# Four pairs of k-tiles by seven products, quarters from GpSimd's queue, and 1 KB runs in the gated transposes

## The chip, the cores and the metric

The kernel runs on one core of one Trainium2 chip. The metric is the device time of one execution in microseconds (us). The version before takes 1965.18 us, the median of three runs (1962.07 to 1971.79).

## What is computed

One decoder layer over 256 tokens of width 2048, all in float32: a half-step SwiGLU feed-forward, a mixer (gated DeltaNet beside stick-breaking attention), a second half-step feed-forward, a gated embedding, and a norm. The change lies in the two feed-forwards and at the kernel's start.

```python
def swiglu(x, w_gu, w_down):
    gate, up = jnp.split(x @ w_gu, 2, axis=-1)
    return (jax.nn.silu(gate) * up) @ w_down

h = h + 0.5 * swiglu(rms_norm(h, ffn1_norm[i]), ffn1_w_gu[i], ffn1_w_down[i])   # D 2048, D_FF 5632
h = h + hybrid_mixer(rms_norm(h, mix_norm[i]), ...)
h = h + 0.5 * swiglu(rms_norm(h, ffn2_norm[i]), ffn2_w_gu[i], ffn2_w_down[i])
gate = jax.nn.sigmoid(rms_norm(h, ple_norm[i]) @ ple_w_gate[i])
h = h + gate * (p[i] @ ple_w_proj[i])
return rms_norm(h, final_norm)
```

## The kernel before

**Float32 by three matmuls.** Each float32 operand is split into a high part (ScalarE casts it to fp32r) and a low part (VectorE subtracts the high part). A product is then three matmuls: high by high, high by low, low by high. The activations `nTh`, `nTl` (and `hTh`, `hTl` between the two layers of a feed-forward) are split once. Each weight is split as it arrives.

**Plain pairs.** `weight_pair` loads two k-tiles of a 512-column block into `raw` from SP's queue (four buffers), ScalarE makes `whi` (L70), VectorE makes `wlo` (L71); three buffers each. A pair takes 12 matmuls: two k-tiles, two halves of the 256 tokens, three matmuls.

**Groups.** A feed-forward is done in three parts (`PARTS`: 3, 4 and 4 blocks of 512 of the inner width). A part has one group for each block ("gu": a gate and an up block, eight pairs of k-tiles each) and then two groups of the second layer ("dn": two output blocks each). A group's first `ns` pairs of k-tiles are not done plainly but by seven products (`Group`): the two k-tiles and two token halves on one side, the two k-tiles and two column blocks on the other, form a two-by-two product, which Strassen's and Winograd's scheme does in seven products in place of eight, so 21 matmuls for a pair of both blocks in place of 24. `ns` is 3 in gu groups (`NS`), and 2 or 3 in dn groups (`NS_DOWN`); two gu groups at the start of the first feed-forward and one of the second are all plain.

**The sums.** The weight side of the seven products (`all_sums`) works in four buffers `R`, the quarters, named by k-tile and column block. Each product's operand is split by ScalarE into `shi` (L282) and by VectorE into `slo` (L283), two buffers each. Between products VectorE adds one quarter to another twice (L287), and GpSimd's queue twice adds a quarter from memory onto a buffer with an accumulating DMA (L291). The activation side is made by `halves`, once a part for gu and once for dn: VectorE adds high and low (L396), forms four sums `S` (L403), ScalarE and VectorE split them into `Sh` (L404) and `Sl` (L405). After the third and fourth product ScalarE copies a bank to `part` and VectorE adds it into another (L321, L322).

**What sets the order.** `plan` writes for each group the order of its plain pairs and, between them, the seven products of the group that follows (`at`), and the loads of the quarters of the group after that (`loads`). `next_weights` walks that list and prepares up to two pairs and one sum ahead. Each engine then works through its own instructions in order. Quarters are loaded from SP's queue, in line with the pairs. At the end of a gu group, `down_input` multiplies gate and up (L426), transposes 32 by 32 blocks on VectorE (L165), and sends them through memory (`scr`, `tT`) to finish the transpose; `hTh` and `hTl` are made from it later.

**The start.** `first_loads` fetches the input's transposed tiles `xT` in step with the first group's pairs, then `h` itself. The first group goes through all eight pairs of the gate block and then through those of the up block.

Of the kernel before, what the change touches and what calls it, by code (L numbers as in the profile page):

```python
# [16 lines left out]
P = 128  # L17
T = 256
# [11 lines left out]
NS = 3  # L30
NS_DOWN = tuple(3 if i1 - i0 == 4 else 2 for i0, i1 in PARTS)


W_IN_ORDER = (2, 0, 4, 3, 1, 5, 8, 10, 12, 9, 11, 13, 6, 7)
EPS = 1e-6
# [4 lines left out]
def block_kernel(ctx, tc, a, out):  # L40
# [37 lines left out]
    def next_weights():  # L78

        ahead = min(LEAD, done[1] // 2)  # L80
# [44 lines left out]
    for _ in range(8):  # L125
        nc.tensor.matmul(idle[:, 0:P], zero[:, 0:P], zero[:, 0:P], start=True, stop=True)
# [70 lines left out]
    def norm_block(nT, which, j, tmp):  # L197

        if j < 3:
            lanes.add(0, norm_block_behind(nT, which, j, tmp))  # L200
            return
# [39 lines left out]
    class Group:  # L241
# [89 lines left out]
    def plan(n):  # L331
# [9 lines left out]
        for p, (i0, i1) in enumerate(PARTS):  # L341
            for i in range(i0, i1):
                src = [sources("w_gu" + n, 2 * i + b) for b in range(2)]
                groups.append(Group("gu", p, [x[0] for x in src], [x[1] for x in src], NS if i > (n == "1") else 0,
# [4 lines left out]
        made = []  # L349
        for i, group in enumerate(groups):  # L350
# [3 lines left out]
            at, loads = [], {}  # L354
# [25 lines left out]
    for nb in range(3):  # L380
        order += [("pair", a["w_pp"][nb])] + [("pair", a["w_pg"][nb][g]) for g in range(KD // 2)]
    order.append(("pair", a["w_pp"][3]))

    def halves(kind, his, los, ns, wait=0):
# [5 lines left out]
        sh = fp.tile([P, 4, NS, P], F32R, tag="Sh", name="Sh")  # L390
        sl = fp.tile([P, 4, NS, P], F32R, tag="Sl", name="Sl")
        for g0 in range(0, ns, 2):
            n = min(2, ns - g0)
            hi, lo = his[g0 // 2], los[g0 // 2]
            x = fp.tile([P, 2, 4, P], F32, tag="tT", name="tT").rearrange("p t q y -> p (t q y)")[:, 0:2 * n * T]
# [871 lines left out]
```

## Time and profile before

| what | value |
|---|---|
| median of the runs | 1965.18 us |
| the profiled execution's own time | 1963.91 us |
| its span, first to last instruction | 1962.2 us |
| mean granted TensorE clock | 0.998 |
| share of the chain that ended last: PE | 87% |
| bytes moved by DMA | 468.28 MB, 239 GB/s on average |

The first feed-forward lies at 0 to about 705 us of the span, the mixer up to about 1165 us, the second feed-forward up to about 1855 us. An instruction's duration in the profile holds the latency of its pipeline, so instructions of one engine that follow each other directly start closer together than their durations say; where the rate matters, the distance of starts is taken. In the tables by stage, a window's row has the busy time of PE, PEld, DVE, ACT and POOL with counts in brackets, then the granted clock, the share of the DMA engines' time that is busy, and GB/s.

### The profile page before, as it was taken

The page shows a single profiled execution, that of the slowest core. Times are in us where ns is not written, and L with a number is a line of the kernel's source. Part 1 is how long each engine was busy: PE and PEld are TensorE (multiplying, and loading weights), DVE is VectorE, ACT ScalarE, POOL GpSimd, SP SyncE. Part 2 cuts the span into 40 slices and gives each one's busy share as a digit, 9 for nine tenths or more (in the row PEclk, how much of TensorE's full clock was granted, in tenths as well). Part 3 has the DMA queues.
Part 4 walks back from the last instruction along what each step waited for, and adds up shares of the span by engine and source line. Part 5 has one row for each costly group of instructions (what it writes and reads, how often), then busy time and mean ns, then how long its engine had stood idle before and what let it go on. Part 6 is the DMA issues. An engine that isn't in the chain of part 4 may idle for free.

```text
span 1962.2 us, 24725 instructions
## 1 busy us (share of the span) xinstructions
PE 1942.3 (99%) x8941; PEld 1606.5 (82%) x8941; DVE 1536.1 (78%) x1771; ACT 1152.7 (59%) x1402; POOL 83.7 (4%) x108
## 2 busy tenths in 40 slices
PE   9999999999999999999999999999999999999998
PEld 7888888888888888878888888887888888888887
DVE  6779878897888766797856578888889887798755
ACT  6655656565656567665555456565566555665554
POOL 0000000000000000010100000000000000000000
PEclk9999999999999999999999999999999999999999
DMA  8988888888887765556564788887889878887764
GB/s 298 293 246 249 265 261 254 261 260 245 264 278 241 223 217 164 175 160 222 168 208 155 242 284 244 255 263 247 251 254 292 274 229 240 258 273 246 235 206 148
DMA packets 166554, 468.28 MB, mean 239 GB/s; under 512 B 20640, under 2 KB 59552, under 8 KB 166304
## 3 DMA queue, kind: packets, MB, share of 16 engines
q1 hardware_dynamic: 156352, 418.57, 62.3%
q0 software_dynamic: 8928, 46.67, 13.4%
q8 instruction: 70, 1.15, 0.2%
q10 hardware_dynamic: 1152, 1.47, 0.2%
q14 instruction: 52, 0.43, 0.1%
HBM read 444.62 MB, written 22.02 MB: 238 GB/s over the span
## 4 chain that ended last, share of the span: by engine, by line
PE 87%; DVE 5%; issue 4%; DMA 2%; ACT 1%; POOL 0%; SPq 0%; ACTq 0%; POOLq 0%; DVEq 0%
PE u L472 5%; PE u L473 5%; PE u L471 5%; PE g L472 5%; PE g L473 5%; PE g L471 5%; PE d L472 4%; PE d L473 4%; PE d L471 4%; PE pj L106 3%; PE pj L107 3%; PE pj L105 3%; PE g L315 3%; PE g L316 2%; PE g L314 2%
## 5 line engine op out<-in xcount | busy, mean ns | idle before, releaser
L70 ACT CAST whi<-raw 128x1024 fp32r<-128x1024 f32 (+1 forms) x531 | 557.2, 1051 | 521.5 <-PE d L473 112.4
L71 DVE TENSOR_TENSOR wlo<-raw,whi 128x1024 fp32r<-128x1024 f32 (+1 forms) x531 | 643.3, 1216 | 220.7 <-ACT whi L70 217.6
L283 DVE TENSOR_TENSOR slo<-R,shi 128x1536 fp32r<-128x1536 f32 (+1 forms) x217 | 365.5, 1686 | 126.6 <-ACT shi L282 124.8
L282 ACT CAST shi<-R 128x1536 fp32r<-128x1536 f32 (+1 forms) x217 | 309.6, 1428 | 166.2 <-PE g L316 44.8
L471 PE MATMUL g<-whi,nTh 128*128 128x512 f32 x476 | 185.3, 391 | 2.3 <-ACT whi L70 2.3
L472 PE MATMUL g<-wlo,nTh 128*128 128x512 f32 x476 | 186.4, 392 | 0.5 <-DVE wlo L71 0.5
L473 PE MATMUL g<-whi,nTl 128*128 128x512 f32 x476 | 186.2, 391 | 0.0
L471 PE MATMUL u<-whi,nTh 128*128 128x512 f32 x476 | 185.2, 389 | 0.0
L472 PE MATMUL u<-wlo,nTh 128*128 128x512 f32 x476 | 185.2, 389 | 0.0
L473 PE MATMUL u<-whi,nTl 128*128 128x512 f32 x476 | 185.2, 389 | 0.0
L105 PE MATMUL pj<-whi,nTh 128*128 128x512 f32 x448 | 179.7, 401 | 0.0
L106 PE MATMUL pj<-wlo,nTh 128*128 128x512 f32 x448 | 175.3, 391 | 2.2 <-DVE wlo L71 2.2
L107 PE MATMUL pj<-whi,nTl 128*128 128x512 f32 x448 | 175.0, 391 | 0.0
L472 PE MATMUL d<-wlo,hTh 128*128 128x512 f32 x448 | 174.4, 389 | 0.0
L471 PE MATMUL d<-whi,hTh 128*128 128x512 f32 x448 | 174.3, 389 | 0.0
L473 PE MATMUL d<-whi,hTl 128*128 128x512 f32 x448 | 174.3, 389 | 0.0
L471 PEld LDWEIGHTS g<-whi,nTh 128*128 128x128 f32 x476 | 89.4, 188 | 21.8 <-ACT whi L70 3.4
L472 PEld LDWEIGHTS g<-wlo,nTh 128*128 128x128 f32 x476 | 89.8, 189 | 20.6 <-DVE wlo L71 1.8
L473 PEld LDWEIGHTS g<-whi,nTl 128*128 128x128 f32 x476 | 89.8, 189 | 18.8 <-DVE nTl L155 0.2
L287 DVE TENSOR_TENSOR R<-R 128x1536 f32<-128x1536 f32 (+1 forms) x62 | 104.4, 1683 | 0.9
L471 PEld LDWEIGHTS u<-whi,nTh 128*128 128x128 f32 x476 | 89.3, 188 | 18.6
L472 PEld LDWEIGHTS u<-wlo,nTh 128*128 128x128 f32 x476 | 89.3, 188 | 18.6
(304 smaller groups left out, 3222.3 us busy)
## 6 DMA issues: line engine op xcount, KB each, us to landing
raw<-in_w_gu SPq DMA_DIRECT2D x220, 512.0 KB, 5.5
raw<-in_w_down SPq DMA_DIRECT2D x112, 512.0 KB, 5.4
raw<-in_w_in SPq DMA_DIRECT2D x112, 512.0 KB, 3.5
R<-in_w_gu2q SPq DMA_DIRECT2D x40, 768.0 KB, 6.0
R<-in_w_gu1q SPq DMA_DIRECT2D x36, 768.0 KB, 6.0
scr<-tb SPq DMA_DIRECT2D x74, 256.0 KB, 4.8
raw<-in_w_out SPq DMA_DIRECT2D x32, 512.0 KB, 4.4
raw<-in_w_pg SPq DMA_DIRECT2D x32, 512.0 KB, 4.3
```

What stands on the lines that cost most here:

```text
L70: nc.scalar.copy(hi[:, j, :], raw[:, j, :])
L71: nc.vector.tensor_tensor(out=lo[:, j, :], in0=raw[:, j, :], in1=hi[:, j, :], op=ALU.subtract)
L105: nc.tensor.matmul(outs[t], xh[:, c], whi[:, j, :], start=st, stop=False)
L106: nc.tensor.matmul(outs[t], xh[:, c], wlo[:, j, :], start=False, stop=False)
L107: nc.tensor.matmul(outs[t], xl[:, c], whi[:, j, :], start=False, stop=sp)
L282: nc.scalar.copy(hi, w)
L283: nc.vector.tensor_tensor(out=lo, in0=w, in1=hi, op=ALU.subtract)
L287: nc.vector.tensor_tensor(out=self.raw[x], in0=self.raw[x], in1=self.raw[y], op=ALU.add)
L315: nc.tensor.matmul(out, xh, wlo[:, g, :], start=False, stop=False, skip_group_check=True)
L471: nc.tensor.matmul(out, xh[:, c], whi[:, j, :], start=st, stop=False, skip_group_check=True)
L472: nc.tensor.matmul(out, xh[:, c], wlo[:, j, :], start=False, stop=False, skip_group_check=True)
L473: nc.tensor.matmul(out, xl[:, c], whi[:, j, :], start=False, stop=sp, skip_group_check=True)
```

## The change

- `NS` goes from 3 to 4 and the 3s of `NS_DOWN` to 4: one more pair of k-tiles by seven products in 19 gu groups and 8 dn groups. Quarters are then 128x2048 in place of 128x1536.
- Quarters are loaded from GpSimd's queue. They no longer have a buffer each by name: a group's quarters go, in the order of their use, into the buffers that the group before leaves first, and three loads are placed after that group's fifth, sixth and seventh product, the fourth at the start of the next group.
- The products stand one plain pair apart from the second (same kind of group) or third pair on, where before they were spread from the third on over all pairs.
- `halves` computes its four sums in place in a `sil` buffer, two pairs at a time, and lays `Sh` and `Sl` out by pair.
- `down_input` has its own transpose: one store of 512 KB and reads in runs of 1 KB, where there were two stores and runs of 512 bytes.
- The first group of the first feed-forward takes its pairs by k-tile, so that gate and up alternate; `xT` is loaded at half the pace, between the `h` loads; the plain groups' weights lie in an array of their own; ten idle matmuls stand at the start in place of eight.
- The embedding's operand is loaded in the last stage, and its matmuls follow the gate's.

```diff
-NS = 3
-NS_DOWN = tuple(3 if i1 - i0 == 4 else 2 for i0, i1 in PARTS)
+NS = 4
+NS_DOWN = tuple(4 if i1 - i0 == 4 else 2 for i0, i1 in PARTS)
...
-            self.raw[j, b] = raw = current[0].tile([P, NS, NB], F32, tag=f"R{j}{b}", name="R")[:, 0:self.ns]
-            nc.sync.dma_start(out=raw, in_=self.quarters[b][j])
-
-        def loads(self):
-            return [("load", lambda j=j, b=b: self.load(j, b)) for j, b in ((0, 1), (1, 0), (0, 0), (1, 1))]
+            self.raw[j, b] = raw = current[0].tile([P, NS, NB], F32, tag=self.home[j, b], name="R")[:, 0:self.ns]
+            nc.gpsimd.dma_start(out=raw, in_=self.quarters[b][j])
+
+        def loads(self, last=None):
+            free = [last.home[q] for q in ((0, 1), (1, 0), (0, 0), (1, 1))] if last else ["R0", "R1", "R2", "R3"]
+            use = (0, 0), (0, 1), (1, 1), (1, 0)
+            self.home = dict(zip(use, free))
+            return [("load", lambda q=q: self.load(*q)) for q in use]
...
             if follower is not None and follower.ns:
-                first = 2 if group.ns else 8
-                at = [first + j * (n_plain - 1 - first) // 7 for j in range(7)]
+                first = 8 if not group.ns else 1 if group.kind == follower.kind else 2
+                at = [min(first + j, n_plain - 1) for j in range(7)]
...
                 if after is not None and after.ns:
-                    for x, one in zip((5, 6, 7, 7), after.loads()):
-                        loads.setdefault(at[x] if x < 7 else min(at[6] + 1, n_plain - 1), []).append(one)
+                    *three, last = after.loads(follower)
+                    for x, one in zip((4, 5, 6), three):
+                        loads.setdefault(at[x], []).append(one)
+                    carried = [last]
...
+            x = fp.tile([P, 2 * NB], F32, tag="sil", name="S")[:, 0:n * NB]
...
+            for o, y, z, op in ((a22, a21, a22, ALU.subtract), (a21, a21, a11, ALU.subtract),
+                                (a11, a22, a11, ALU.subtract), (a12, a11, a12, ALU.add)):
+                nc.vector.tensor_tensor(out=o, in0=y, in1=z, op=op)
+            sx = [y[:, g0:g0 + n].rearrange("p g j t y -> p (g j t y)") for y in (sh, sl)]
+            nc.scalar.copy(sx[0], x)
+            nc.vector.tensor_tensor(out=sx[1], in0=x, in1=sx[0], op=ALU.subtract)
...
+                tb = fp.tile([P, 4, 2, P], F32, tag="tT", name="tb")
+                for t in range(2):
+                    nc.vector.transpose(tb[:, :, t].rearrange("p c (j x) -> p c j x", j=4),
+                                        sil[:, t, :].rearrange("p (j c x) -> p c j x", j=4, c=4))
+                yield
+                scr = dr.tile([P, 4, 2, P], F32, tag="scr2", name="scr2", bufs=2)
+                nc.sync.dma_start(out=scr, in_=tb)
...
+        xs_at = {2 * k - 1 if k < 4 else k + 3: 2 * k for k in range(1, KD // 2)}
+        for i in range(1, 16):
+            if i in xs_at:
+                load_x(xs_at[i])
+            if 5 <= i < 13:
+                t, j = todo[i - 5]
                 nc.sync.dma_start(out=h[:, t, block(j)], in_=a["x"][t * P:(t + 1) * P, block(j)])
```

How this moves instructions, at three places.

GpSimd's instructions from the program's start, before: the identity is made, and the first DMA is an accumulating one (L291) in the middle of the second group.

```order
L130 MEMSET fill 128x64
masks.py:197 MEMSET ident 128x128
masks.py:199 ISA
masks.py:199 AFFINE_SELECT ident<-ident 128x128
L235 TENSOR_TENSOR rstd_515<-rstd,mhalf 128x2
L291 DMA R<-in_w_gu1q 128x1536 x2
```

And of the change, where L271 is the load of a quarter and L298 the accumulating DMA.

```order
L132 MEMSET fill 128x64
masks.py:197 MEMSET ident 128x128
L271 DMA R<-in_w_gu1q 128x2048
masks.py:199 ISA
masks.py:199 AFFINE_SELECT ident<-ident 128x128
L271 DMA R<-in_w_gu1q 128x2048 x3
L298 DMA R<-in_w_gu1q 128x2048
```

The four loads of the first quarters, which stood on SP's queue behind the second group's pairs, now stand ahead of everything that GpSimd waits for.

VectorE's instructions from the start in the change (`nTl` is the input's low part, `slo` the low part of the first product's weights):

```order
L157 SCALAR_TENSOR_TENSOR nTl<-xT,gains,nTh 128x256
L73 TENSOR_TENSOR wlo<-raw,whi 128x512 x2
L157 SCALAR_TENSOR_TENSOR nTl<-xT,gains,nTh 128x256
L290 TENSOR_TENSOR slo<-R,shi 128x2048
L73 TENSOR_TENSOR wlo<-raw,whi 128x1024
```

The split of the first quarter now stands ahead of the second plain pair's, although its product comes a group and a half later.

VectorE in the last gu group of the second part of the first feed-forward, where the next group is a dn group, before (rows from the pair that comes third from the group's start; `S` and `Sl` belong to `halves`):

```order
L71 TENSOR_TENSOR wlo_2779<-raw_2777,whi_2778 128x1024
L165 STREAM_TRANSPOSE tb_2803<-sil_2603 128x512
L165 STREAM_TRANSPOSE tb_2804<-sil_2603 128x512
L283 TENSOR_TENSOR slo_2825<-R_2703,shi_2824 128x1536
L71 TENSOR_TENSOR wlo_2820<-raw_2818,whi_2819 128x1024
L287 TENSOR_TENSOR R_2703<-R_2703,R_2705 128x1536
L403 TENSOR_TENSOR S_2845<-tT_2843 128x128 x2
L403 TENSOR_TENSOR S_2845<-S_2845,tT_2843 128x128
L71 TENSOR_TENSOR wlo_2854<-raw_2852,whi_2853 128x1024
```

The same place in the change, from the third pair (`wlo_2715`) on:

```order
L73 TENSOR_TENSOR wlo_2715<-raw_2713,whi_2714 128x1024
L294 TENSOR_TENSOR R_2575<-R_2575,R_2617 128x2048
L451 STREAM_TRANSPOSE tb_2749<-sil_2550 128x4x128 x2
L73 TENSOR_TENSOR wlo_2764<-raw_2762,whi_2763 128x1024
L424 TENSOR_TENSOR S_2754<-hTh_2105,hTl_2106 128x1024
L290 TENSOR_TENSOR slo_2769<-R_2575,shi_2768 128x2048
L430 TENSOR_TENSOR S_2754<-S_2754 128x2x128
L294 TENSOR_TENSOR R_2575<-R_2575,R_2657 128x2048
L430 TENSOR_TENSOR S_2754<-S_2754 128x2x128
L73 TENSOR_TENSOR wlo_2797<-raw_2795,whi_2796 128x1024
L430 TENSOR_TENSOR S_2754<-S_2754 128x2x128
L73 TENSOR_TENSOR wlo_2841<-raw_2839,whi_2840 128x1024
```

From `wlo_2715` to the split of the fifth product of the dn group (`slo_2913`), which ends the stretch that the prediction weighs, VectorE has 34 instructions besides the first: 7 `wlo`, 4 `slo`, 2 `R`, 2 sums of high and low, 8 `S`, 2 `Sl`, 3 transposes, 2 `sil`, 2 adds of banks and 2 `hTl`. Between the first uses of the two on PE stand 120 matmuls of 512 columns.

More of the change, by code (lines that the diff above doesn't have):

```diff
@@ L380, in block_kernel @@
     for nb in range(3):
-        order += [("pair", a["w_pp"][nb])] + [("pair", a["w_pg"][nb][g]) for g in range(KD // 2)]
+        order += [("pair", a["w_pg"][nb][g]) for g in range(KD // 2)] + [("pair", a["w_pp"][nb])]
     order.append(("pair", a["w_pp"][3]))
@@ L500, in ffn @@
                         hTl.append(tl)
-                        gen = down_input(outs, sil, th, tl)
+                        gen = down_input(outs, sil, th, tl, 2 if len(hTh) == PARTS[group.part][1] else 3)
                         next(gen)
```

105 lines of the change are left out of this document (55 added, 50 removed).

## The prediction

> **What bounds the kernel now.** I read the page's first rows, then the order of time on PE at one spot, to see what one matmul costs.
>
> ```profile
> span 1962.2 us, 24725 instructions
> ...
> PE 1942.3 (99%) x8941; PEld 1606.5 (82%) x8941; DVE 1536.1 (78%) x1771; ACT 1152.7 (59%) x1402; POOL 83.7 (4%) x108
> ```
>
> ```profile
> 563.46 0.39 PE L314 MATMUL u<-shi,Sh 128*128 128x512 f32 x1
> ...
> 564.82 0.39 PE L314 MATMUL u<-shi,Sh 128*128 128x512 f32 x1
> ```
>
> PE is busy for 99% of the span, so the bound is the number of matmuls. The row says 0.39 us for one, but that holds its latency: six matmuls start between 563.46 and 564.82, so one costs 0.227 us, and 12 (a plain pair, or a product of ns 4) cost 2.72 us. VectorE is second with 78%. Where it fills a stage, PE falls behind; the table by stage shows this (PE's busy time is the second number, VectorE's the fourth):
>
> ```profile
> 180.00:200.00 20.00, 19.26 (x84) 15.28 (x84) 19.34 (x20) 12.32 (x13) 1.74 (x2) 1.00 0.68 197
> 200.00:220.00 20.00, 19.52 (x86) 15.83 (x85) 15.14 (x14) 11.15 (x11) 0.00 (x0) 1.00 0.85 274
> 340.00:360.00 20.00, 20.00 (x90) 16.57 (x89) 18.94 (x22) 11.58 (x11) 1.76 (x2) 1.00 0.79 211
> 1340.00:1360.00 20.00, 19.12 (x83) 15.10 (x82) 19.75 (x22) 13.27 (x14) 0.86 (x1) 1.00 0.91 256
> ```
>
> At 180 to 220 and at 1340 us, where the first part of a feed-forward ends, VectorE is at 97 to 99% and PE loses 0.74 + 0.48 and 0.88 us, 2.1 in all. At 340 us, where a dn group is prepared, VectorE has 1.06 us left in 20.
>
> **The change, part by part.**
>
> *Matmuls.* A further pair of k-tiles by seven products saves 24 - 21 = 3 matmuls in each of 19 gu and 8 dn groups: 81 x 0.227 = **-18.4 us**, all on the bounding engine. Two more idle matmuls end before the first weight is there: nothing; on the path they would cost under 1 us.
>
> *VectorE's work.* Rows of the groups, kept apart by shape:
>
> ```profile
> L71 DVE TENSOR_TENSOR wlo<-raw,whi 128x1024 fp32r<-128x1024 f32 x529 | 641.9, 1218 | 219.4 <-ACT whi L70 216.2 <-DMA tT<-scr 1.5
> L283 DVE TENSOR_TENSOR slo<-R,shi 128x1536 fp32r<-128x1536 f32 x189 | 331.5, 1755 | 122.9 <-ACT shi L282 122.4
> L287 DVE TENSOR_TENSOR R<-R 128x1536 f32<-128x1536 f32 x54 | 94.6, 1752 | 0.8
> L283 DVE TENSOR_TENSOR slo<-R,shi 128x1024 fp32r<-128x1024 f32 x28 | 34.0, 1222 | 3.7 <-ACT shi L282 2.4
> L322 DVE TENSOR_TENSOR d<-d,part 128x512 f32<-128x512 f32 x48 | 32.1, 691 | 4.7 <-PE d L316 3.5 <-ACT part L321 1.2
> L435 DVE TENSOR_TENSOR hTl<-tT,hTh 128x512 fp32r<-128x512 f32 x44 | 28.3, 684 | 1.1 <-ACT hTh L434 1.1
> L403 DVE TENSOR_TENSOR S<-S,tT 128x256 f32<-128x256 f32 x24 | 10.0, 416 | 0.1
> L396 DVE TENSOR_TENSOR tT<-hTh,hTl 128x1024 f32<-128x1024 f32 x6 | 7.3, 1224 | 0.2
> L405 DVE TENSOR_TENSOR Sl<-S,Sh 128x1024 fp32r<-128x1024 f32 x12 | 14.6, 1218 | 1.2 <-ACT Sh L404 1.2
> ```
>
> From 1024 to 1536 columns a split grows by 0.53 us, so one of 2048, which the trace lacks, is estimated at 2.29 us; linear growth fits all the shapes, and I keep no other value. A group loses two plain pairs (-2.44) and its seven splits and two adds of quarters grow by 9 x 0.53 = 4.8: **+2.4 us of VectorE for -0.68 us of PE**. In 27 groups that is +64 us. `halves` grows too: two rounds of 1.22 + 4 x 0.416 + 1.22 = 8.2 us, where one full and one half round took 6.6.
>
> How much fits is read where VectorE runs without a break:
>
> ```profile
> 340.07 1.76 DVE L287 TENSOR_TENSOR R<-R 128x1536 f32<-128x1536 f32 x1
> 341.75 1.22 DVE L71 TENSOR_TENSOR wlo<-raw,whi 128x1024 fp32r<-128x1024 f32 x1
> 342.88 1.22 DVE L405 TENSOR_TENSOR Sl<-S,Sh 128x1024 fp32r<-128x1024 f32 x1
> 344.02 1.40 DVE L426 SCALAR_TENSOR_TENSOR sil<-u,rstd,sil 128x512 f32<-128x512 f32 x2
> 345.34 1.21 DVE L71 TENSOR_TENSOR wlo<-raw,whi 128x1024 fp32r<-128x1024 f32 x1
> 346.47 1.30 DVE L165 STREAM_TRANSPOSE tb<-sil 128x512 f32<-128x512 f32 x2
> 347.69 1.72 DVE L283 TENSOR_TENSOR slo<-R,shi 128x1536 fp32r<-128x1536 f32 x1
> ```
>
> ```profile
> 346.08 0.39 PE L472 MATMUL g<-wlo,nTh 128*128 128x512 f32 x1
> ```
>
> The starts are 1.13 us apart after a 1024 split, 1.68 after a 1536, 0.66 for a `sil`, 0.61 for a transpose: 0.085 us less than the durations. So in a dense stretch a 2048 operation costs 2.20, a 1024 one 1.13, a `hTl` or an add of banks 0.60, an `S` 0.33.
>
> An even run of gu groups stays below the bound: 8 x 1.13 + 9 x 2.20 + 4 x 0.60, and 3.8 for `sil`, transposes and `hTl`, are 35.0 us, against 180 x 0.227 = 40.9 of PE. I cost it at nothing; the cover is 5.9 us a group.
>
> The end of a part is another matter (**place A**, four times: two parts with ns 4 in each feed-forward). In the 34 instructions counted in the section on the change VectorE needs 7 x 1.13 + 4 x 2.20 + 2 x 2.20 + 4 x 1.13 (sums and `Sl`) + 8 x 0.33 + 3 x 0.61 + 2 x 0.66 + 4 x 0.60 = 33.8 us. PE has 120 x 0.227 = 27.2 us of matmuls there. VectorE is ahead when the stretch begins, by as much as the buffers allow: the weights of the third plain pair in a run were ready at 341.75 + 1.22 = 342.97 us and used at 346.08, so 3.1 us. The rest, 33.8 - 27.2 - 3.1 = 3.5 us, PE waits: 4 x 3.5 = **14 us**. Bounds: nothing, if the lead were 6.6 us; 26 us, if it were none. I take the measured lead.
>
> Where the dn groups of a part give way to the next gu group (**place B**, four times), the trace already has a loss of 1.2 us at 180 to 220. There five splits and two adds grow by 7 x 0.53 = 3.7 and `halves` by 1.6, and PE has 5 x 0.68 = 3.4 more to do meanwhile: 1.9 more, so 3.1 us, twice. At the second such boundary PE loses nothing today, and I take half of it, 1.5, twice: 9.2 in all (bounds 0 and 20). Less the 2.1 lost today, A and B add **+21 us** (bounds -2 and +44).
>
> *The start.* DMA shares by stage (last two numbers of a row), and a wait of today:
>
> ```profile
> 10.00:20.00 10.00, 9.34 (x33) 7.28 (x34) 9.19 (x15) 7.75 (x12) 0.00 (x0) 0.83 0.94 342
> 20.00:30.00 10.00, 10.00 (x46) 8.18 (x45) 9.07 (x16) 6.94 (x12) 0.00 (x0) 1.00 0.93 306
> 30.00:40.00 10.00, 10.00 (x46) 8.29 (x45) 5.50 (x5) 6.47 (x13) 0.00 (x0) 1.00 0.98 315
> 40.00:50.00 10.00, 10.00 (x46) 8.29 (x45) 3.92 (x6) 7.29 (x12) 0.71 (x1) 1.00 0.86 289
> 50.00:60.00 10.00, 10.00 (x46) 8.29 (x45) 8.40 (x9) 5.66 (x6) 0.00 (x0) 1.00 0.98 374
> ...
> 57.54 7.25 DMA raw<-in_w_gu
> ```
>
> The DMA engines are nearly full from 10 us on, and the first group needs 16 pairs of 0.524 MB, 2.1 MB of `xT` and 2.1 MB of `h`: 12.6 MB before it ends. The four quarters, 4.2 MB, now start beside them, since nothing on GpSimd's queue holds them back. At 306 to 374 GB/s, 4.2 MB are 11 to 14 us, and today's reserve is four raw buffers, 2.1 MB or 6 us. With 16.8 MB at 340 GB/s in place of a last pair due at 47 us I take **+4 us**, net of the wait at 57.54, behind four loads of quarters, which goes. Bounds: 0 (taking pairs by k-tile lets `xT` come at half the pace) and 14.
>
> The Trainium skill, "DMA: Bandwidth & Descriptors", section "Issuing engines are not separate DMA queues", says that transfers from different engines share the same 16 DMA engines, so that another queue saves issue time alone. By that rule the 4 us stand; were GpSimd's queue bandwidth of its own, the sum would be 4 us lower; the full shares above speak for the rule.
>
> *Quarters and accumulating DMAs.*
>
> ```profile
> R<-in_w_gu2q SPq DMA_DIRECT2D x40, 768.0 KB, 6.0
> R<-in_w_gu2q POOLq DMA_DIRECT2D x20, 768.0 KB, 8.5
> R<-in_w_down10q POOLq DMA_DIRECT2D x4, 512.0 KB, 6.8
> L291 POOL DMA_DIRECT2D R<-in_w_gu2q x20 | 17.4, 869 | 369.4 <-DVE R L287 198.9 <-DVE slo L283 124.7 <-ACT Sh L404 24.7
> ```
>
> An accumulating load grows by 1.7 us for 256 KB, so 1 MB takes about 10.2 us, after 0.87 of issue. The one that follows the third product's split must land before the sixth is split, six items or 16.3 us of PE later; the sixth's two splits take 1.9 (ScalarE, grown as VectorE's) + 2.3. So 16.3 - 0.9 - 10.2 - 4.2 = 1.0 us are to spare with no lead, about 4 with today's: nothing. Six issues a group are 5.2 us of GpSimd in 41. A quarter's load waits for the split that empties its buffer; behind it on GpSimd stands only an accumulating load that waits for a later split anyway. A quarter is loaded some eight items (22 us) before its use, against 6 us of landing: hidden.
>
> *Costed at nothing:* the 1 KB runs and the fewer stores (transposed blocks are used a group later; without that cover, some us per part), 54 fewer `raw` loads and 124 quarters off SP's queue, the embedding moved behind the gate, `split_p`. ScalarE has about 29 us of work in a group of 41.
>
> **The sum**, against the profiled execution's own 1963.9 us (the median of the runs is 1.3 above it): 1963.9 - 18.4 + 21 + 4 = 1970.5, so **1971 us**.
>
> **The rivals.**
>
> *VectorE's backlog is hidden.* If it enters place A with twice the lead, A and B stay as they are. For it: further on, pairs have more time in their three buffers, and PE loses nothing at 340 us with VectorE at 95%. Against it: the losses at 180 and 1340 us. Then 1963.9 - 18.4 + 4 = 1950 us.
>
> *The accumulating load comes too late.* At places A and B the third product's split is late, so the lead is gone and 1.0 us is all there is; the load begins to decide where landing takes over 11.2 us, and down quarters scaled from 6.8 us at 512 KB, beside 1 MB loads on the same queue, may well take 12.5. Then each of eight places, with some two groups each, waits 1.3 us less what is shared: about +12, so 1983 us. This ends slower than before.
>
> Here also belongs a rule of the Trainium skill that speaks against GpSimd's queue: "SBUF — State Buffer", section "SBUF: two separate sides", says that GpSimd cannot write descriptors while VectorE holds the port they share; its part "A bandwidth-pool intuition that's wrong" gives 620 ns that become 3100. If it held here, an issue of 0.87 would become an estimated 4 us and the 1.0 us to spare would be gone everywhere; the sum would pass 1983. The trace speaks against it: 869 ns on average beside a VectorE that is 80 to 95% busy.
>
> **How the numbers follow.** Forecast, 1960 to 1976: 0.45. Hidden backlog, about 1950: 0.22. Late accumulation or a larger backlog, 1977 and more: 0.33. A measurement of this kernel tells about 0.5% from no change, so 1955 and 1975 are the borders: faster 0.22, same 0.43, slower 0.35. For the range I take 1949 (A and B free, the start at 3) to 1990 (A and B at +35 of the +44 bound, the start at 10).
>
> **What would show it.** The matmul count falls by 81. In the windows around the ends of parts, VectorE shows over 19.5 of 20 us and PE 16 to 18; PE's waits name `slo` splits, some 3 us a place. In the even gu runs PE stays at 20.0. In the first 55 us DMA shares stay near 1.0 and PE loses 4 to 5 us more. If PE waits for an accumulating DMA, the second rival holds; if its losses at the ends of parts are below 1 us, the first. The prediction is wrong altogether if 2048-wide operations cost other than 2.29 us, or if the even runs lose time.

## The result and the profile after

The changed kernel takes 2035.88 us (median of 4 runs, 2026.65 to 2039.5) against 1967.62 us for the one before in the same session: a ratio of 1.0356, 95% interval 1.0330 to 1.0381. It is slower by 68 us, where 1971 us had been forecast. The profiled execution took 2039.5 us.

The page of the changed kernel, its span, the engines' busy time, the granted clock in 40 slices, two DMA queues (q1 is SP's, q0 is GpSimd's), and the chain that ended last:

```profile
span 2037.8 us, 24233 instructions
...
PE 1964.1 (96%) x8864; PEld 1606.3 (79%) x8864; DVE 1609.9 (79%) x1717; ACT 1171.7 (57%) x1348; POOL 154.0 (8%) x232
...
PEclk8999999999989999999999999999999999998999
...
q1 hardware_dynamic: 114112, 296.92, 42.2%
q0 software_dynamic: 26784, 182.46, 32.6%
...
PE 72%; DVE 10%; DMA 8%; issue 6%; ACT 3%; SPq 1%; POOL 0%; ACTq 0%; POOLq 0%; DVEq 0%
DMA tT<-scr 4%; PE u L504 4%; PE u L505 4%; PE u L503 4%; PE d L505 3%; PE g L504 3%; PE g L503 3%; PE d L504 3%; PE d L503 3%; PE g L505 3%; PE pj L108 3%; PE pj L107 3%; PE pj L109 3%; PE g L322 3%; PE g L323 3%
```

Two things to see: PE has fewer matmuls and yet falls from 99% to 96% of a longer span, so it waits; and the first line on the chain is no matmul but a DMA, the read of a transposed tile back from memory. The tables of waits name who stood for it, before and after (us in total, times, longest):

```profile
ACT hTh L434 <- DMA tT<-scr: 5.1, 5, 1.3
```

```profile
ACT hTh L466 <- DMA tT<-scr: 63.6, 15, 10.1
ACT whi L72 <- DMA raw<-in_w_gu: 23.9, 10, 4.7
PE d L321 <- ACT shi L289: 19.7, 14, 4.0
PE g L321 <- ACT shi L289: 10.7, 3, 3.9
```

PE itself mostly waits for ScalarE's casts `shi`. ScalarE works in order, so whoever keeps it at `hTh` keeps back every weight cast behind.

To place the losses I add up, over all matmuls, by how much the start of one lies more than 0.227 us behind the start of the one before. Steps of under 0.01 us are left out. That **loss** was 23.5 us before (some 12 of them in the mixer) and is 114.0 us after. The 90.5 us more, less the 77 matmuls that the trace has fewer (17.5 us), make 73 of the 75.6 us by which the span grew. It lies in five kinds of places. The table by stage shows the start, one end of a part (380 to 420 us) and one run of even gu groups (540 to 580 us):

```profile
0.00:20.00 20.00, 10.73 (x34) 7.80 (x34) 6.80 (x12) 7.38 (x10) 3.08 (x11) 0.74 0.90 341
...
380.00:400.00 20.00, 17.13 (x71) 12.73 (x70) 18.76 (x23) 13.12 (x13) 1.12 (x2) 1.00 0.74 236
400.00:420.00 20.00, 16.95 (x73) 13.25 (x73) 16.14 (x13) 9.38 (x9) 1.95 (x3) 0.98 0.93 272
540.00:560.00 20.00, 20.00 (x90) 16.49 (x88) 11.92 (x9) 7.68 (x7) 1.44 (x2) 1.00 0.85 207
560.00:580.00 20.00, 14.56 (x50) 11.12 (x48) 13.82 (x12) 13.06 (x12) 1.63 (x3) 0.74 0.78 287
```

| place | loss before | loss after | predicted to be added |
|---|---|---|---|
| start, 0 to 80 us | 6.3 | 21.2 | 4 |
| ends of parts (A): 380-440, 640-700, 1560-1620, 1820-1880 | 0 | 41.3 | 14 |
| dn to gu boundaries (B): 180-220, 460, 1340-1400 | 3.5 | 2.7 | 7 |
| even gu runs: 540-600, 1520, 1740 | 0 | 26.8 | 0 |
| mixer and ends of feed-forwards | 13.6 | 22.0 | 0 |

At 560 us PE has 50 matmuls in 20 us where 90 would fit, and VectorE is at 13.82: no backlog there. The chain of waits from 535 to 568 us tells what happened (start, us, what), and after it GpSimd's and PE's rows in order of time:

```profile
540.04 7.64 DMA scr<-tb
...
549.08 12.07 DMA tT<-scr
...
561.22 0.09 ACT hTh L466
...
562.36 1.81 ACT shi L289
...
564.19 2.30 DVE slo L290
```

```profile
535.40 0.88 POOL L298 DMA_DIRECT2D R<-in_w_gu1q  x1 [8.02 <-DVE R L294]
546.96 0.87 POOL L298 DMA_DIRECT2D R<-in_w_gu1q  x1 [10.69 <-DVE slo L290]
551.33 0.56 POOL L271 DMA_DIRECT2D R<-in_w_gu1q  x1 [3.50 <-DVE slo L290]
```

```profile
564.21 0.80 PE L321 MATMUL g<-shi,nTh 128*128 128x512 f32 x1 [3.90 <-ACT shi L289]
566.54 0.80 PE L322 MATMUL g<-slo,nTh 128*128 128x512 f32 x1 [1.53 <-DVE slo L290]
567.13 0.63 PE L323 MATMUL g<-shi,nTl 128*128 128x512 f32 x1
567.56 0.63 PE L321 MATMUL g<-shi,nTh 128*128 128x512 f32 x1
```

The store of the transposed blocks runs beside one accumulating load of GpSimd's queue (L298) and lands after 7.6 us. SP waits for it, then issues the four reads at 547.7, just behind a second accumulating load (546.96), with a quarter's load (551.33) to follow. The last of the reads lands 12 us after its issue. ScalarE has waited 10.1 us, PE then waits 3.9 and 1.5, and its next matmuls start 0.43 us apart, at about half the clock.

### The profile page after: what moved, and what is told of

The parts are those of the page before. It is cut to its first block, busy times and chain, and to the rows that moved or that the text cites. A ratio compares the mean times of both kernels' runs of the same rounds, so it can differ in the third digit from the quotient of the medians.

```text
span 2037.8 us, 24233 instructions
## 1 busy us (share of the span) xinstructions
PE 1964.1 (96%) x8864; PEld 1606.3 (79%) x8864; DVE 1609.9 (79%) x1717; ACT 1171.7 (57%) x1348; POOL 154.0 (8%) x232
## 3 DMA queue, kind: packets, MB, share of 16 engines
q0 software_dynamic: 26784, 182.46, 32.6%
## 4 chain that ended last, share of the span: by engine, by line
PE 72%; DVE 10%; DMA 8%; issue 6%; ACT 3%; SPq 1%; POOL 0%; ACTq 0%; POOLq 0%; DVEq 0%
DMA tT<-scr 4%; PE u L504 4%; PE u L505 4%; PE u L503 4%; PE d L505 3%; PE g L504 3%; PE g L503 3%; PE d L504 3%; PE d L503 3%; PE g L505 3%; PE pj L108 3%; PE pj L107 3%; PE pj L109 3%; PE g L322 3%; PE g L323 3%
## 5 line engine op out<-in xcount | busy, mean ns | idle before, releaser
L72 ACT CAST whi<-raw 128x1024 fp32r<-128x1024 f32 (+1 forms) x477 | 499.4, 1049 | 425.0 <-PE pj L109 108.2
L73 DVE TENSOR_TENSOR wlo<-raw,whi 128x1024 fp32r<-128x1024 f32 (+1 forms) x477 | 577.2, 1215 | 193.5 <-ACT whi L72 191.9
L290 DVE TENSOR_TENSOR slo<-R,shi 128x2048 fp32r<-128x2048 f32 (+1 forms) x217 | 465.0, 2148 | 109.8 <-ACT shi L289 108.4
L289 ACT CAST shi<-R 128x2048 fp32r<-128x2048 f32 (+1 forms) x217 | 389.6, 1801 | 203.9 <-DVE R L294 61.2
L294 DVE TENSOR_TENSOR R<-R 128x2048 f32<-128x2048 f32 (+1 forms) x62 | 132.7, 2141 | 0.3
L108 PEld LDWEIGHTS pj<-wlo,nTh 128*128 128x128 f32 x448 | 84.3, 188 | 22.3 <-DVE wlo L73 6.4
L321 PE MATMUL g<-shi,nTh 128*128 128x512 f32 x228 | 91.5, 401 | 10.7 <-ACT shi L289 10.7
L109 PEld LDWEIGHTS pj<-whi,nTl 128*128 128x128 f32 x448 | 84.1, 188 | 17.6
L322 PE MATMUL g<-slo,nTh 128*128 128x512 f32 x228 | 92.2, 404 | 5.9 <-DVE slo L290 5.9
L107 PEld LDWEIGHTS pj<-whi,nTh 128*128 128x128 f32 x448 | 84.1, 188 | 17.4 <-ACT whi L72 1.0
```

Of the source, the lines that this page charges most:

```text
L72: nc.scalar.copy(hi[:, j, :], raw[:, j, :])
L73: nc.vector.tensor_tensor(out=lo[:, j, :], in0=raw[:, j, :], in1=hi[:, j, :], op=ALU.subtract)
L107: nc.tensor.matmul(outs[t], xh[:, c], whi[:, j, :], start=st, stop=False)
L108: nc.tensor.matmul(outs[t], xh[:, c], wlo[:, j, :], start=False, stop=False)
L109: nc.tensor.matmul(outs[t], xl[:, c], whi[:, j, :], start=False, stop=sp)
L289: nc.scalar.copy(hi, w)
```

## The experiments

Each kernel is the changed one with one edit or a sum of edits. "Loss" is that of the whole execution, as above. Sessions differ by some us, so differences under 5 us between two runs aren't read, only those against the kernel before.

| run | us | ratio to before, 95% | loss, us | ScalarE's wait for tT at hTh, us |
|---|---|---|---|---|
| the changed kernel | 2035.9 | 1.0356 (1.0330-1.0381) | 114.0 | 63.6 |
| e1_2kb_runs | 2046.4 | 1.0416 (1.0384-1.0448) | 121.3 | 66.5 |
| e2_two_more_steps | 2035.9 | 1.0372 (1.0345-1.0400) | 109.2 | 58.1 |
| e3_first_quarters_from_sp | 2016.7 | 1.0270 (1.0227-1.0313) | 99.4 | 67.6 |
| e4_all_quarters_from_sp | 2004.5 | 1.0216 (1.0181-1.0251) | 78.5 | 59.2 |
| f1_sums_not_in_sil | 2024.2 | 1.0316 (1.0297-1.0335) | 95.9 | 69.0 |
| f2_no_trip_through_memory | 1992.3 | 1.0153 (1.0138-1.0168) | 66.9 | none |
| f3_sums_apart_and_quarters_from_sp | 2008.8 | 1.0234 (1.0219-1.0249) | 87.0 | 73.7 |
| f4_three_pairs | 1982.6 | 1.0099 (1.0079-1.0119) | 40.5 | 3.0 |
| g3_second_sum_by_vector | 2011.7 | 1.0243 (1.0218-1.0267) | 87.5 | 24.1 |
| g4_and_first_quarters_from_sp | 1991.3 | 1.0138 (1.0109-1.0167) | 70.9 | 25.8 |
| g1_three_edits | 1983.8 | 1.0109 (1.0093-1.0124) | 58.1 | 36.8 |
| g2_all_quarters_from_sp_too | 1964.6 | 1.0014 (1.0002-1.0026) | 41.4 | 10.9 |
| h1_sums_back_in_sil | 1983.7 | 1.0106 (1.0083-1.0129) | 60.7 | 12.8 |
| h2_dn_groups_with_three | 1958.3 | 0.9977 (0.9966-0.9988) | 28.4 | 7.6 |
| h3_dn_products_a_pair_later | 1961.1 | 0.9988 (0.9973-1.0003) | 40.8 | 2.7 |

### Why tT comes late: e1, e2, e4

The first guess (theory T) was that the two queues take turns packet by packet, so that SP's short runs crawl beside 8 KB packets.

```diff
-    m[name + "q"] = np.ascontiguousarray(b[:, :ns].transpose(0, 3, 2, 1, 4))
+    m[name + "q"] = np.ascontiguousarray(b[:, :ns].transpose(0, 3, 1, 2, 4))
...
-                nc.gpsimd.dma_start(out=self.raw[x], in_=self.quarters[y[1]][y[0]], accum_op=ALU.add)
+                nc.gpsimd.dma_start(out=self.raw[x], in_=self.quarters[y[1]][y[0]].rearrange("g p n -> p g n"), accum_op=ALU.add)
```

> The quarters lie in memory so that GpSimd's queue moves them, loads and accumulating loads, in runs of 2 KB in place of 8 KB; nothing else differs from the changed kernel (2035.9 us). Theory T, packets take turns: a DMA engine serves GpSimd's and SP's queue packet by packet, so that SP's runs of 1 KB (the last reads of the gated transposes), 2 KB (xT) and 4 KB (weights) advance by one for each 8 KB packet. With 2 KB packets ScalarE's wait for tT falls from 63.6 us to under 20, the matmuls of the first 60 us lose under 15 in place of 21, and the time is 1975 to 2005. Theory W, the transpose has too few steps whatever the queues do: the wait stays at 50 to 70 us, the time at 2025 to 2045. Theory B, VectorE's backlog at the ends of parts, as predicted: 2025 to 2045 too. If GpSimd's four times as many descriptors cost more than they bring, the accumulating loads land after more than 13 us and the time is above 2045.

Measured: 2046.4 us, the wait for tT at 66.5. The time is also above every range but the last, whose sign (landing after more than 13 us) did not show: the quarters' median time to landing rose from 8.5 to 9.3 us. The runs did not become as short as planned everywhere: in the trace the accumulating loads come in packets of 2 KB and the plain loads in packets of 4 KB, in place of 8. The size of GpSimd's runs, as far as it was changed, is not the lever, and that form of the theory falls.

```diff
-    gen = down_input(outs, sil, th, tl, 2 if len(hTh) == PARTS[group.part][1] else 3)
+    gen = down_input(outs, sil, th, tl, 2 if len(hTh) == PARTS[group.part][1] else 5)
```

> The cast of the transposed tile waits five steps in place of three after its reads are issued (in all but the last group of a part, where it stays at two). Of the 63.6 us that ScalarE waited for tT, 48.6 lie in those groups and 15.0 in the last ones. Theory W (the cast is placed too early) and theory T (the reads are slowed by packets that take turns) both expect the wait to fall to 15 to 20 us and the time by 30 to 50 us, to 1985 to 2005, since a stall of the matmuls and the spell at half clock behind it go together. Under theory S, the weights that stand on SP's queue behind the slow reads are late anyway, the wait for tT only turns into ScalarE's wait for raw, and the time stays above 2020. Theory B: no change, 2030 to 2042.

This run decides nothing: ScalarE's instructions stand in the same order in both programs (VectorE's differ in 12 places of 1717), so the cast was not moved. It is all but the changed kernel once more, and its 2035.9 us say how well a time repeats.

```diff
-            nc.gpsimd.dma_start(out=raw, in_=self.quarters[b][j])
+            nc.sync.dma_start(out=raw, in_=self.quarters[b][j])
```

> All loads of quarters go to SP's queue, at the changed places; only accumulating loads stay on GpSimd's. Theory T: ScalarE's wait for tT falls to under half of 63.6 us, since two thirds of the 8 KB packets no longer take turns with the reads but stand behind or ahead of them; what is left comes from the accumulating loads. But a load now holds SP's queue until VectorE has emptied its buffer (GpSimd waited 4.7 us on average at such a load), so the weights behind it come later: the time is 1990 to 2035, and ScalarE's wait for raw grows above 24 us. Theory W: the wait for tT stays at 50 us or more and the time is 2035 or above.

The time came as expected (2004.5), the wait for tT did not: 59.2 us. With only accumulating loads left on GpSimd's queue the reads are as late as before: in the trip of 524 to 542 us one passes beside the store and one beside the reads, as in the changed kernel. Of the 31 us gained 19 lie at the start (e3); that the rest comes from loads that no longer pass beside SP's weights is argued, not shown.

### What the trip through memory costs: f2, g3, f4

```diff
-                tb = fp.tile([P, 4, 2, P], F32, tag="tT", name="tb")
+                tT = fp.tile([P, 4, 2, P], F32, tag="tT", name="tT")
                 for t in range(2):
-                    nc.vector.transpose(tb[:, :, t].rearrange("p c (j x) -> p c j x", j=4),
+                    nc.vector.transpose(tT[:, :, t].rearrange("p c (j x) -> p c j x", j=4),
...
-                nc.sync.dma_start(out=scr, in_=tb)
...
-                    nc.sync.dma_start(out=tT[32 * c:32 * c + 32].rearrange("x q t i -> x q (t i)"),
-                                      in_=scr[:, c].rearrange("(q x) t i -> x q (t i)", q=4))
```

> The gated product is transposed by 32 by 32 blocks on VectorE straight into tT; the store to memory and the reads back are left out, so that hTh and hTl are computed from blocks that stand in the wrong places. All casts, subtractions and matmuls stay. Theory T, the trip comes back late beside GpSimd's transfers: ScalarE's wait for tT of 63.6 us goes, and with it the losses of the matmuls at 540 to 580, 1520 and 1740 us (25.8 us) and about half of those at 400 to 430, 660 to 680, 1600 and 1860 us (some 15 us): 1985 to 2002 us. If the trip is covered and the losses come from VectorE's and ScalarE's own work (theories B and M): 2020 us or more.

It came out at 1992.3 us, in the range of theory T. At 540 to 600, 1520 and 1740 us nothing is lost any more:

```profile
560.00:580.00 20.00, 20.00 (x90) 16.57 (x89) 17.50 (x13) 11.62 (x11) 1.41 (x2) 1.00 0.75 232
```

So the trip costs 43.5 us in the changed kernel. The start (21 us) and a loss of 4 to 6 us at each end of a part stay. Then one of the two accumulating loads was taken from the places where a trip runs:

```diff
             elif i == 2:
-                add_loaded((0, 0), (1, 0))
+                (add if self.by_vector else add_loaded)((0, 0), (1, 0))
...
+            group.by_vector = i > 1 and groups[i - 2].kind == "gu" and (group.kind == "gu" or group.nb == 2)
```

> In 16 groups whose sums are made while tT is read back (the gu groups from the third of a part on, and the second dn group of a part) the third sum, quarter (0,0) plus quarter (1,0), is made by VectorE from the buffers in place of an accumulating load of GpSimd's queue. Otherwise the changed kernel (2035.9 us). Theory A, accumulating loads are what the reads of tT stand behind: in the changed kernel the cast came 4.4 to 6.9 us after the reads were issued where up to 1.4 MB of GpSimd's queue passed meanwhile, and 9 to 13.9 us where 1.8 to 4.2 MB did. With 1 MB less there, ScalarE's wait for tT falls from 63.6 to 15 to 35 us and the time to 2000 to 2020 us. Theory L, any load on GpSimd's queue does it: the quarters' loads move up into the place, the wait stays above 50 us and so does the time, 2030 to 2040 us. Theory B, VectorE is the bound: 16 more additions of 2.2 us make it slower, 2040 to 2060 us.

Measured: 2011.7 us and a wait of 24.1 us, both in the range of theory A. The DMA issues from 540 to 565 us (KB each, median us to landing), of the changed kernel and then of this run:

```profile
R<-in_w_gu1q POOLq DMA_DIRECT2D x2, 1024.0 KB, 10.2
raw<-in_w_gu SPq DMA_DIRECT2D x4, 512.0 KB, 12.9
...
tT<-scr SPq DMA_DIRECT2D x4, 128.0 KB, 10.6
```

```profile
raw<-in_w_gu SPq DMA_DIRECT2D x5, 512.0 KB, 5.6
R<-in_w_gu1q POOLq DMA_DIRECT2D x2, 1024.0 KB, 6.4
...
tT<-scr SPq DMA_DIRECT2D x4, 128.0 KB, 2.8
```

The same four reads take 2.8 in place of 10.6 us, and the weights behind them 5.6 in place of 12.9. So the second accumulating load made them late at this place. VectorE, which does the sum now, delays nothing there: PE is at 20.00 of 20 us from 540 to 580.

That only an accumulating load does this, as theory A has it against theory L, is not shown. The quarters' loads did not move up beside these reads: the next is issued at 554.1 us, when three of the four reads have landed. Where two plain loads of quarters do stand beside the reads, at the four ends of parts, the reads are as late as ever in g3 too. Here are the issues from 659 to 662.5 us. Those of GpSimd's queue are plain loads (L271), and its next accumulating load is issued at 669.99 us, when the reads have been under way for 9 us:

```profile
R<-in_w_down12q POOLq DMA_DIRECT2D x2, 1024.0 KB, 9.2
tT<-scr SPq DMA_DIRECT2D x4, 128.0 KB, 10.5
```

So reads come late behind quarters on GpSimd's queue of either kind, plain or accumulating.

The third run asks whether the fourth pair matters for this.

```diff
-NS = 4
-NS_DOWN = tuple(4 if i1 - i0 == 4 else 2 for i0, i1 in PARTS)
+NS = 3
+NS_DOWN = tuple(3 if i1 - i0 == 4 else 2 for i0, i1 in PARTS)
```

> The change with three pairs of k-tiles by seven products as before, all the rest of it kept (queues, buffers, spacing of the products, transposes, start). 81 matmuls more, 18.4 us. If the fourth pair is what costs (theory B: VectorE's and ScalarE's larger splits, 1 MB accumulating loads), the losses of the matmuls outside the mixer fall from about 100 to under 40 us: 1985 to 2005 us. If the costs are those of the queue, the shared buffer and the start, they stay: 2035 to 2055 us.

With three pairs the same queues, buffers and transposes cost little: 1982.6 us, a wait for tT of 3.0 us. The trace shows one reason. Of the 88 reads of `tT` in the feed-forwards, 31 are issued in the changed kernel while GpSimd's queue has a quarter under way, and they land after a median of 9.5 us, the other 57 after 3.0; with three pairs only 3 are. The loss is 40.5; against before it has 7 us more at the start and 6 more at the mixer's start, and nothing at the ends of parts. So the new arrangement by itself costs about 20 us, and the fourth pair, which was to save 18.4, costs 53 more in it.

### The start: e3

```diff
-            nc.gpsimd.dma_start(out=raw, in_=self.quarters[b][j])
+            (nc.gpsimd if self.behind else nc.sync).dma_start(out=raw, in_=self.quarters[b][j])
...
+            self.home, self.behind = dict(zip(use, free)), last is not None
```

> The four first quarters of each feed-forward are loaded from SP's queue, in line with the weights, as before the change; all others stay on GpSimd's queue. The matmuls of the first 60 us lost 21.2 us against 5.3 before. Theory T and the prediction's start term in its larger form: the loss falls to 5 to 9, the time by 12 to 16 us to 2020 to 2025. If the pairs by k-tile and the slower xT cause the loss at the start, it stays and the time does too (2032 to 2040). Nothing changes after 60 us under either.

Measured: 2016.7 us, 19 less, somewhat more than expected (the four times lie between 2007 and 2025); the loss up to 80 us falls from 21.2 to 4.1, so pairs by k-tile and the slower `xT` are not its cause. The DMA issues of the first 40 us, of the changed kernel and then of this run:

```profile
R<-in_w_gu1q POOLq DMA_DIRECT2D x5, 1024.0 KB, 10.9
xT<-in_xT SPq DMA_DIRECT2D x7, 256.0 KB, 10.6
```

```profile
xT<-in_xT SPq DMA_DIRECT2D x7, 256.0 KB, 7.2
```

### The buffer that sums and silu share: f1, f3, g4, g1

At the ends of parts PE waits twice, always for the same time. ScalarE's and PE's rows from 386 us:

```profile
387.80 1.27 ACT L472 ACTIVATE sil<-g,rstd 128x512 f32<-128x512 f32 x2 [1.48 <-DVE Sl L433]
389.05 1.91 ACT L289 CAST shi<-R 128x2048 fp32r<-128x2048 f32 x1
391.01 0.50 PE L321 MATMUL d<-shi,Sh 128*128 128x512 f32 x1 [1.07 <-ACT shi L289]
393.28 0.50 PE L321 MATMUL d<-shi,hTh 128*128 128x512 f32 x1 [1.78 <-ACT shi L289]
```

The silu writes the `sil` buffer, and `halves` forms its sums `S` in that buffer: the silu must wait until VectorE has read `S` for the last time (`Sl`), and `shi` stands behind the silu.

```diff
-            x = fp.tile([P, 2 * NB], F32, tag="sil", name="S")[:, 0:n * NB]
+            x = act.tile([P, NB], F32, tag="nat", name="S", bufs=4)
```

> The four sums S of halves are formed one pair of k-tiles at a time in nat buffers, in place of two pairs at a time in the one sil buffer that gate's silu also needs. Otherwise the changed kernel (2035.9 us). Theory M, the shared buffer: at the four places where a part ends, ScalarE's silu waits for the last read of S (1.48 us at 386 to 388 us), and the casts shi behind it come late, so that the matmuls wait 1.07 and then 1.78 us (at 391, 656, 1574, 1840 us alike). These waits go: 4 x 2.85 = 11 us and the spells at a lower clock behind them, 2015 to 2026 us. Theory B, VectorE has too much to do there, as predicted: the waits stay or grow, since VectorE gets 4 x 8 more small operations: 2034 to 2045 us. Theory T, GpSimd's queue: no change at these places.

Measured: 2024.2 us; the pairs of waits of 1.07 and 1.78 us are gone at all four places. (In f2, which has no trip, all four are there, unchanged, so the two causes are separate.) What the edit brings depends on the rest:

> The last two edits that should help, together: the sums S in nat buffers, and all loads of quarters on SP's queue (alone 2004.5 us). If theory M holds and adds up with theory T, the waits of 1.07 and 1.78 us at the ends of parts go as well: 1985 to 1996 us. If the two share their places or theory B holds: 2000 to 2012 us.

> The run with VectorE's third sum, and the first quarters from SP's queue as well (alone 2016.7 us, 19 us gained). Under theory A the two add up: 1980 to 2002 us. If the third sum on VectorE brought nothing: 2012 to 2025 us.

> VectorE's third sum, the first quarters from SP's queue, and the sums S in nat buffers (alone 12 us gained). If the three causes are separate (accumulating loads, start, shared buffer), it comes to 1965 to 1990 us, and the matmuls lose 30 to 60 us outside the mixer in place of about 100. If VectorE is what is left at the ends of parts (theory B), the losses there stay at 4 x 8 us and more: 1990 to 2010 us.

With all quarters from SP it brought nothing that can be told (f3: 2008.8 against 2004.5, intervals that overlap): the wait for tT is 73.7 us there, and that it hides the gain is argued, not shown. The hope that the two add up failed. The third sum on VectorE and the start do add up (g4: 1991.3, 20 us under g3, 25 under e3), and with the sums apart it is 1983.8 (g1).

### What is left: g2, h1, h2, h3

> As the run of three edits, but with every load of a quarter on SP's queue (with the S edit but without VectorE's third sum: 2008.8 us). Theory A: one accumulating load is left beside the reads, as before the change, the wait for tT falls from 73.7 us to under 30, and the time is 1968 to 1992 us. If loads that hold SP's queue for VectorE's splits are what costs there: 2000 us or more.

1964.6 us, level with the kernel before (1.0002 to 1.0026), and the clock is 0.998 again. 71 of the changed kernel's us are accounted for by these edits, yet the 81 matmuls saved bring nothing. The loss is 41.4 us, and 16.3 of it lie at the four ends of parts (4.4, 3.3, 6.0 and 2.7). The stage table there:

```profile
600.00:620.00 20.00, 18.60 (x81) 14.75 (x80) 18.24 (x22) 13.92 (x15) 0.88 (x1) 1.00 0.89 236
1500.00:1520.00 20.00, 18.71 (x82) 15.03 (x81) 18.39 (x23) 13.66 (x15) 0.86 (x1) 1.00 0.88 213
```

VectorE is at 18.2 to 18.4 of 20 us, and PE waits for `Sh` (5.6 us in all, four times), `slo` (3.8) and `hTl` (2.3). The last two are VectorE's. The waits for `Sh` are not, as ScalarE's and PE's rows at one of the four places show:

```profile
611.30 1.14 ACT L466 CAST hTh<-tT 128x512 fp32r<-128x512 f32 x2 [1.69 <-DMA tT<-scr]
612.35 0.61 ACT L431 CAST Sh<-S 128x512 fp32r<-128x512 f32 x1
613.01 0.50 PE L321 MATMUL d<-shi,Sh 128*128 128x512 f32 x1 [1.40 <-ACT Sh L431]
```

`Sh` stands behind `hTh`, for which ScalarE has waited 1.6 to 2.0 us at each of the four places because `tT` was not back: this is the trip once more.

Three runs start from g2. The first takes the edit of the sums back, the second sets `NS_DOWN` to 3 in place of 4, the third begins the first dn group's products one pair later.

```diff
-NS_DOWN = tuple(4 if i1 - i0 == 4 else 2 for i0, i1 in PARTS)
+NS_DOWN = tuple(3 if i1 - i0 == 4 else 2 for i0, i1 in PARTS)
```

```diff
-                first = 8 if not group.ns else 1 if group.kind == follower.kind else 2
+                first = 8 if not group.ns else 1 if group.kind == follower.kind else 3 if group.kind == "gu" else 2
```

> The kernel of 1964.6 us (S in nat buffers, all quarters from SP's queue, VectorE's third sum) with S back in the sil buffer. Theory M: the waits of 1.07 and 1.78 us at four places come back and those of 1.3 to 1.7 us for Sh go, and clock spells with them: 1970 to 1982 us. If the S edit costs as much as it brings once the rest is mended: 1961 to 1968 us.

1983.7 us: the shared buffer is worth 19 us once the trip is in time, more than theory M's upper end, since the two waits and the clock spells come back at every end of a part.

> The kernel of 1964.6 us with three pairs of k-tiles by seven products in the dn groups (four stay in the gu groups): 24 matmuls more, 5.4 us. Theory B, VectorE's backlog at the ends of parts is what is left: the losses there, about 16 us in four places (4.4, 3.3, 6.0 and 2.7), fall by more than half, and the time is 1955 to 1963 us. If the backlog isn't the cause: 1968 to 1973 us.

1958.3 us, with 24 matmuls more. The losses at the ends of parts fall from 16.3 to 0.8 us, as theory B forecast (elsewhere they rise by 2.5):

```profile
600.00:620.00 20.00, 20.00 (x88) 16.23 (x87) 17.29 (x18) 14.44 (x16) 0.87 (x1) 1.00 0.98 317
1500.00:1520.00 20.00, 20.00 (x88) 16.24 (x87) 18.22 (x22) 15.58 (x18) 0.86 (x1) 1.00 0.89 277
```

So the fourth pair in the dn groups is what costs there. That it does so by VectorE's work alone is not shown: the edit also shortens ScalarE's casts and the loads of the quarters, and at 1500 us VectorE is hardly less busy (18.22 in place of 18.39). This version beats both kernels, by 0.23% (0.12 to 0.34) against before.

> The kernel of 1964.6 us with the products of the first dn group of a part begun a pair of weights later; the last of them then follow each other without a pair between. Theory: Sh comes 5 us earlier for its use, its waits of 1.3 to 1.7 us at six places go: 1955 to 1962 us. Theory B: the backlog only moves to the end of the group, where products stand close, and PE waits for slo there: 1964 to 1975 us.

1961.1 us, not to be told from the kernel before or, by the session's scatter, from g2. The time lies in the range of the first theory (1955 to 1962), and PE's four waits for `Sh` are gone; but the loss of the profiled execution is 40.8, no less than g2's: it moved to waits for `hTl` (4.9 us) and `slo` (5.6), as theory B has it. So neither is decided.

## Why the prediction was wrong

**Matmuls, -18.4.** Right: the run with three pairs (f4) has 81 more than the changed kernel. Against before the trace has 77 fewer, 17.5 us, since the change adds some elsewhere, the two idle ones among them. VectorE's estimate for 2048 columns (2.29 us) was right as well: `slo` takes 2.30 in the row above.

**"Costed at nothing: the 1 KB runs and the fewer stores (transposed blocks are used a group later)".** This step failed, together with "a quarter's load ... hidden". At 540 us ScalarE reached the casts some 11 us after the store was issued (551 against 540 us), not a group of 41 later, and the trip took 21. I asked of each accumulating load only whether its own user would have it in time, and that it did. What it does to SP's transfers beside it I left at nothing: four reads of 128 KB went from 2.8 to 10.6 us, and 43.5 us hang on the trip (f2), while 24.2 go when one accumulating load of two is taken away in 16 groups (g3). The even gu runs, "costed at nothing; the cover is 5.9 us a group", lost 26.8 us by this and not by VectorE.

The Trainium skill has the rule that I did not weigh: "DMA: Bandwidth & Descriptors", section "Queues, rings and completion order", says that each DMA engine goes round the queues that have work, a packet of several descriptors at a time. The section I used says that transfers of all engines interleave on the same DMA engines, and I took from it only that a second queue adds no bandwidth. The lateness of SP's reads beside GpSimd's transfers agrees with the rule. e1 does not settle it: shorter runs changed nothing, which fits turns of as many bytes as before, and no run shows where such a packet ends.

**The start, +4.** The mechanism was right (e3), the size wrong: 14.9 us of loss, just over the upper bound of 14. The 4 was not worked out either: 16.8 MB at 340 GB/s are 49.4 us, 2.4 behind the 47. In the first 60 us ScalarE waits 9.2 us for `raw` and 6.4 for `xT`, which took 10.6 us to land, against 3.3 and nothing in e3; whether the four `raw` buffers that I counted on were filled by then was not followed.

**Place A, +14.** 41 us. Three causes share it. VectorE's backlog, the only one that the term had, is there, and its size is near by luck in part: with the other two mostly mended these places lose 16.3 us (g2, where some of VectorE's 16 added sums lie too), but only 6.1 us of PE's waits in that run are for VectorE's `slo` and `hTl`, and 5.6 for `Sh`, which the trip holds up. The loss goes when dn groups have three pairs (h2). The other two causes I had not seen: the late trip of the part's last group, and the silu that waits for `S` in the shared buffer (1.07 and 1.78 us, four times, and what follows). The diff showed the shared tag; I counted the operations and not who waits for the buffer.

**Place B, +7 net.** Too much: these boundaries lose 2.7 us, less than before.

**The rivals.** VectorE's backlog is not hidden (g2, h2). The accumulating load landed after a median of 9.1 us (`w_gu`), not 10.2, and in time for the sum that needs it (ScalarE's waits for `R` from the feed-forwards stay below 3 us a row); it made others late. The rule of the Trainium skill that the second rival weighs, on GpSimd's descriptor writing, had no part here: an accumulating load still takes 0.87 to 0.88 us to issue in the rows above.

**The clock.** No term of the sum had it. Matmuls that start 0.40 to 0.52 us apart cost 27.0 us beyond 0.227 in the changed kernel and 4.5 before: a quarter of what was added.

What stays open: why the sums in `nat` brought 12 us in one setting (f1), nothing in another (f3), 7 in a third (g1) and 19 in a fourth (h1) was followed only as far as the waits; why fewer reads fall beside GpSimd's loads with three pairs was not asked; and the 8 us more around the mixer were not tried.

## What to carry to other kernels

When bulk transfers move to another queue, price them for their neighbours and not only for their users: list each short transfer that a full engine's queue waits for in order, and what will pass beside it. Before a buffer is shared, name who writes it next and what stands behind that writer. And judge a saving by the stage in which it lands: in the dn groups the fourth pair cost more than it saved. The version that keeps it in the gu groups alone (h2) is the only one below the kernel before, though no run took it away just there.

## What the runs showed of the hardware that was not expected

Two waits of 1.07 and 1.78 us, with one matmul between them, were enough for matmuls at about half rate: in the changed kernel 2.1 to 3.4 us of them follow at three of the four places (1.0 to 1.6 us lost), and none at the fourth (391 us). 5.5 us (13 matmuls, 2.6 us lost) follow the waits of 3.9 and 1.5 us at 564. So in these cases short waits cost about half their length once more.

An accumulating load weighs more than its bytes. In e4, where GpSimd's queue has nothing else, 1 MB lands after a median of 9.4 to 9.6 us, and a plain load of the same size from SP's queue after 6.7 (the queues' rows have packets, MB and the share of the engines' time):

```profile
q1 hardware_dynamic: 131968, 418.57, 59.4%
q0 software_dynamic: 8928, 60.82, 16.7%
...
R<-in_w_gu2q SPq DMA_DIRECT2D x40, 1024.0 KB, 6.7
...
R<-in_w_gu2q POOLq DMA_DIRECT2D x20, 1024.0 KB, 9.6
```

Of e4's span of 2001 us that is 5.5 us of all the DMA engines for each MB of GpSimd's queue and 2.8 for SP's. In the changed kernel GpSimd's queue moves 121.6 MB of plain loads besides. Its 32.6% of 2037.8 us leave them an estimated 2.7 us a MB, so it is the accumulating that costs twice, and not the queue.
